# An encoder block on one core: four chunks of the conditioning weight summed in the branch stage, the first by one-row products, and the first norm's modulation through PSUM

## The chip, the cores and the metric

The kernel runs on one core of a Trainium2 chip. A core has four compute engines, each with its own in-order queue: TensorE (PE) multiplies matrices into PSUM, VectorE (DVE) and ScalarE (ACT) work on SBUF and PSUM, GpSimd (POOL) on SBUF. SyncE (SP) issues the DMAs, in order too. The metric is the device time of one execution in microseconds; the median of several runs is compared. Before the change it is 1581.42 us (three runs, 1576.99 to 1583.48).

## The reference, cut to what matters

One encoder layer with D = 1024, S = 1024 positions, batch 1, in float32. Six vectors of 1024 elements, made from a conditioning vector c, scale, shift and gate the stream:

```python
ada = jax.nn.silu(c) @ w_ada[i] + b_ada[i]            # (1024) @ (1024, 6144)
shift1, scale1, gate1, shift2, scale2, gate2 = jnp.split(ada, 6, axis=-1)
h = rmsnorm(x, g_mix[i]) * (1 + scale1) + shift1
proj = h @ w_in[i]                                    # q, k, v of two attentions, two gates
...
merged = jax.nn.sigmoid(ga) * ya + jax.nn.sigmoid(gb) * yb
x = x + gate1 * (merged @ w_out[i])
h2 = rmsnorm(x, g_ffn[i]) * (1 + scale2) + shift2
u = depthwise_conv_seq(h2 @ w_up[i], conv_w[i], conv_b[i])
...
x = x + gate2 * ((jax.nn.gelu(u_gate, approximate=True) * u_val) @ w_down[i])
return rmsnorm(x, g_final)
```

So shift1 and scale1 are needed before the first projection, gate1 at the output projection, shift2 and scale2 at the second norm, gate2 only at the very end.

## The kernel before

Everything is kept transposed: features on the 128 partitions, in KT = 8 blocks k, and positions along the free dimension, in two halves of 512. A float32 product is made of three fp32r products, from operands that were split into a high part (ACT rounds a copy) and a low part (the rest, by DVE or POOL): L77 to L79 for 512 columns, L247 to L249 for the 256-column v products. The stages, in order of time: start (norm1, first q, k and v products), v stage (the rest of v for both attentions), two attentions with the gate projections, branch stage (both branch products, gates, merge), output projection, norm2, the wide feed-forward products, the end.

**w_ada.** It is 24 MB and comes as 12 chunks j of 512 columns, each [128, 8, 512], in four tiles of two rows t (512 KB). A chunk is a sum over 8 rows, each scaled by a column of cs (silu of c, one value per partition), then a sum over partitions. `ada_rows` (L155, L157) does the sum over rows on DVE, in place; `ada_sums` (L141) turns each 128 columns into a column of PSUM by a product with `ones`, or with a column of cs where a row was not scaled; it is 4 products, 8 records in a profile, to a tile named pada. `ada_bias` adds the bias. Chunks 0 to 3 hold shift1 and scale1, chunk q those for k = 2q and 2q + 1, so that norm1 can go on in four steps. Chunks 4 and 5 hold gate1, 6 and 7 shift2, 8 and 9 scale2, 10 and 11 gate2.

**The start** is written out by hand for all engines (`manual_schedule`). ACT squares x's half 0, DVE adds the squares, PE sums them over partitions (L91), `norm_bcast` makes the reciprocal root and PE spreads it over partitions as `pb` in PSUM (L104). Chunk 0 is summed by ACT and POOL for three rows (`ada_rows_pool`), by DVE for four, joined by `ada_join`, with the eighth row by PE from the unscaled weights. `to_sbuf` (L201) copies pb for POOL, `scale_x` (L206) multiplies x by it on DVE or POOL, and `modulate` makes h from a scaled x: its high part on ACT (L212, scale and bias), the full value on DVE (L214) and the low part (L215). Four steps q follow, each with a chunk's sums, two k of modulation, the q and k products of these (`qk_products`, 12 products of 512 columns) and the v products (24 of 256). Their weights are split in two halves by `qk_split` and `v_split` on ACT, POOL and DVE. Half 1 of x is loaded in step 3, then squared and modulated in the same manner.

**The v stage.** After the hand-written block the planner orders the instructions, by its own estimate of times; on each engine that order is then fixed. For both attentions (br) and both halves of v's columns (hv) there are eight products of 128 positions, each copied out by ACT and written to memory (L255); more copies in memory rearrange v for the attentions (L457, L459, L481). Chunks 4 and 5 stand at the end of the hand-written block, and in the loop over (br, hv) two more follow each time, 6 to 11. Their tiles come from a pool of four buffers ("wada", 4 KB per partition).

**The branch stage** is written out by hand for all engines too: 16 iterations i (8 output blocks m, two halves). Each issues the loads of gates i + 2 (a tile of three) and of a block of x, on even i the weights of m + 2; ACT does the sigmoid of gates i + 1; PE makes 2 x 12 products into two banks of PSUM, "pj", of which there are six; DVE multiplies the first with one gate (L821), the second with the other (L822), adds (L823), and ACT and DVE split the sum into m's high and low part (L55, L56). The operands come from `o_operands`, which loads 8 tiles for each branch through four buffers, "oraw", and splits each into its parts on ACT and DVE.

## Time and profile before

| | us |
|---|---|
| median of the runs | 1581.42 |
| profiled execution, its own time | 1584.16 |
| span of that execution's trace | 1582.3 |
| PE busy in the first 205 us | 161.78 |
| PE busy in the branch stage, 725 to 809 us | 84.00 |
| DVE busy in the branch stage | 43.65 |

The profile is of one execution; times within it count from its first instruction. A row of the timeline or of a group names the source line, the engine, the operation, and the tiles written and read; x8 is a count of instructions, and what stands in brackets at the end is the idle time of the engine before it, with what ended it. The chain of waits goes back from the last instruction, at each step to what released it; "issue" there is time for which the profile shows no cause. A window's row has the busy time and the count of each engine, the clock that TensorE was granted (1.00 is full), the share of time that the DMA engines were busy and the rate in GB/s. A busy PE can be at half rate: then a product of 512 columns follows the last after 0.43 us, at full rate after 0.23.

### The profile page before, as it was taken

To read this page: it belongs to the slowest core of one execution; us is meant where nothing else is said; L and a number is where in the kernel's file an instruction comes from. 1 tells how busy PE (TensorE), PEld (TensorE's weight loads), DVE (VectorE), ACT (ScalarE), POOL (GpSimd) and SP (SyncE) were. 2 spreads that over 40 slices of the span, in tenths; PEclk is the share of its full clock that TensorE was granted. 3 is DMA by queue.
4 is the path that set the end of the run, shared out by engine and by line. 5 is a ranking of instruction groups with operands and counts; after the bars stand their busy time and mean duration, and the time that the engine had idled before them with its cause. 6 is when DMAs were issued, how large, how long until landed. Compare 5 with 4: busy or idle time off the path is not lost.

```text
span 1582.3 us, 21932 instructions
## 1 busy us (share of the span) xinstructions
PE 1502.5 (95%) x7884; PEld 1284.6 (81%) x7884; DVE 1046.1 (66%) x1872; ACT 815.1 (52%) x1463; POOL 837.1 (53%) x523
## 2 busy tenths in 40 slices
PE   4897989999999999999999899999999999999998
PEld 3797978888888989888888777788888887778788
DVE  6876455676757667544433899876666667887765
ACT  4531165766676677654335354444444446575542
POOL 4562052535344575521246758676666665678711
PEclk9898989999999999999999999999999999999998
DMA  6747832222223344446534212222222223533313
GB/s 230 263 148 276 273 104 69 85 72 79 82 70 120 103 126 132 148 161 226 187 139 160 94 53 80 93 95 80 80 80 82 90 75 141 168 118 122 112 54 107
DMA packets 113268, 196.86 MB, mean 124 GB/s; under 512 B 40072, under 2 KB 61448, under 8 KB 113160
## 3 DMA queue, kind: packets, MB, share of 16 engines
q1 hardware_dynamic: 112888, 195.20, 37.2%
q8 instruction: 62, 1.02, 0.3%
q14 instruction: 46, 0.38, 0.1%
q10 hardware_dynamic: 272, 0.26, 0.1%
HBM read 158.73 MB, written 42.47 MB: 127 GB/s over the span
## 4 chain that ended last, share of the span: by engine, by line
PE 75%; DVE 12%; ACT 4%; issue 3%; DMA 2%; POOL 2%; SPq 1%; DVEq 0%; ACTq 0%; POOLq 0%
PE pj L885 10%; PE pj L886 10%; PE pj L884 10%; PE pj L77 9%; PE pj L78 9%; PE pj L79 9%; PE pj L402 2%; DVE big L1080 2%; PE pv L249 2%; PE pv L247 2%; PE pv L248 2%; PE O L716 2%; PE T L704 1%; PE S L683 1%; PE O L571 1%
## 5 line engine op out<-in xcount | busy, mean ns | idle before, releaser
L56 POOL TENSOR_TENSOR wlo<-wraw,whi 128x1024 fp32r<-128x1024 f32 (+2 forms) x78 | 180.3, 2311 | 273.4 <-ACT whi L55 229.5
L77 PE MATMUL pj<-h,whi 128*128 128x512 f32 x448 | 180.4, 404 | 8.5 <-ACT h L212 6.7
L78 PE MATMUL pj<-h,whi 128*128 128x512 f32 x448 | 180.7, 403 | 2.2 <-DVE h L215 2.1
L79 PE MATMUL pj<-h,wlo 128*128 128x512 f32 x448 | 180.3, 402 | 0.0
L56 POOL TENSOR_TENSOR wsl<-big,wsh 128x1024 fp32r<-128x1024 f32 (+1 forms) x45 | 110.0, 2447 | 47.9 <-ACT wsh L55 47.8
L1080 DVE SCALAR_TENSOR_TENSOR big<-wc,sm,big 128x256 f32<-128x256 f32 (+1 forms) x132 | 119.1, 950 | 17.3 <-ACT big L1074 17.2
L55 ACT ACTIVATE whi<-wraw 128x1024 fp32r<-128x1024 f32 (+2 forms) x81 | 81.2, 1003 | 87.3 <-PE pj L78 45.3
L77 PEld LDWEIGHTS pj<-h,whi 128*128 128x128 f32 x448 | 85.8, 192 | 24.5 <-ACT h L212 7.0
L78 PEld LDWEIGHTS pj<-h,whi 128*128 128x128 f32 x448 | 86.0, 192 | 18.2 <-DVE h L215 3.2
L79 PEld LDWEIGHTS pj<-h,wlo 128*128 128x128 f32 x448 | 85.9, 192 | 15.8
L542 ACT ACTIVATE P<-P,st 128x256 f32<-128x256 f32 x128 | 64.4, 504 | 45.9 <-DVE st L541 45.0
L541 DVE CUSTOM_DVE_ANT_0 P<-S,bias 128x256 f32<-128x256 f32 x128 | 51.8, 421 | 51.4 <-PE S L588 37.3
L157 DVE SCALAR_TENSOR_TENSOR wada<-wada,cs 128x512 f32<-128x512 f32 x67 | 64.9, 969 | 30.5 <-DMA wada<-w_ada 28.5
L429 POOL TENSOR_SCALAR kl<-kl 64x512 fp32r<-64x512 f32 x32 | 63.5, 1983 | 33.1 <-DVE kl L427 30.2
L1080 DVE SCALAR_TENSOR_TENSOR big<-pj,sm,big 128x512 f32<-128x512 f32 x132 | 67.8, 564 | 16.4 <-ACT big L1074 16.4
L1074 ACT ACTIVATE big<-wc,sm 128x512 f32<-128x512 f32 x44 | 35.8, 817 | 76.3 <-DVE wc L897 45.9
L247 PE MATMUL pv<-vwh,h 128*128 128x256 f32 x256 | 74.6, 292 | 0.0
L249 PE MATMUL pv<-vwh,h 128*128 128x256 f32 x256 | 74.4, 291 | 0.0
L248 PE MATMUL pv<-vwl,h 128*128 128x256 f32 x256 | 73.3, 287 | 0.0
L56 POOL TENSOR_TENSOR wsl<-wraw,wsh 128x768 fp32r<-128x768 f32 (+1 forms) x23 | 49.9, 2168 | 43.8 <-ACT wsh L55 43.8
L474 POOL TENSOR_TENSOR vv<-vv 96x256 fp32r<-96x256 f32 (+2 forms) x32 | 41.0, 1292 | 51.9 <-ACT vv L473 47.6
L694 POOL TENSOR_SCALAR P<-P,stb 128x288 f32<-128x288 f32 (+1 forms) x32 | 39.4, 1231 | 53.6 <-DVE stb L691 41.8
(365 smaller groups left out, 4928.2 us busy)
## 6 DMA issues: line engine op xcount, KB each, us to landing
wada<-w_ada SPq DMA_DIRECT2D x47, 512.0 KB, 5.5
wraw<-w_in SPq DMA_DIRECT2D x36, 512.0 KB, 4.3
big<-w_up SPq DMA_DIRECT2D x22, 512.0 KB, 5.2
wraw<-w_up SPq DMA_DIRECT2D x22, 512.0 KB, 3.6
as<-big SPq DMA_DIRECT2D x22, 512.0 KB, 2.9
big<-as SPq DMA_DIRECT2D x22, 512.0 KB, 6.0
wraw<-w_down SPq DMA_DIRECT2D x24, 384.0 KB, 4.2
gs<-gs SPq DMA_DIRECT2D x32, 256.0 KB, 2.0
```

The costliest lines, as they stand in the source:

```text
L55: act.activation(hi, raw, AF.Copy)
L56: lo_eng.tensor_tensor(lo, raw, f(hi), OP.subtract)
L77: pe.matmul(psum, whi[:, k0 + k], mhi, start=k == 0, stop=False)
L78: pe.matmul(psum, whi[:, k0 + k], mlo, start=False, stop=False)
L79: pe.matmul(psum, wlo[:, k0 + k], mhi, start=False, stop=k == n - 1)
L247: pe.matmul(p, hhi, hi[:, k], start=fresh and k == 0, stop=False, skip_group_check=True)
L248: pe.matmul(p, hhi, lo[:, k], start=False, stop=False, skip_group_check=True)
L249: pe.matmul(p, hlo, hi[:, k], start=False, stop=k == KT - 1, skip_group_check=True)
L884: pe.matmul(psum, whi[:, k], bhi, start=j < 4 and k == 0, stop=False, skip_group_check=True)
L885: pe.matmul(psum, whi[:, k], blo, start=False, stop=False, skip_group_check=True)
L886: pe.matmul(psum, wlo[:, k], bhi, start=False, stop=k == n - 1, skip_group_check=True)
L1080: dve.scalar_tensor_tensor(y[:, dst], src, wt, y[:, dst], OP.mult, OP.add)
```

## The change

- Chunk 0 is summed by PE: `ada_gemv` takes a column of cs as stationary operand and a float32 row of w_ada, 512 columns, as moving one, and adds eight of them into one row of a PSUM bank, `grow`. ACT copies that row to SBUF, and four products with one row of contraction turn it into pada's columns. In PE's queue the first two stand ahead of the square sums, two between these and the transposes of `norm_bcast`, four behind.
- In chunks 1 to 3 DVE sums rows 0 to 4, and PE takes rows 5, 6 and 7 unscaled (three more products of `ada_sums` for each 128 columns). ACT's and POOL's part and the joins are gone.
- `modulate` starts from the unscaled x: DVE writes x times (1 + scale) g times pb to a PSUM bank (two banks in turn, `stages1`), ACT makes the high part from it with the shift as bias, and DVE the low part in one operation. `scale_x` and `to_sbuf` are gone. All of it is on DVE and ACT; the low parts of the first q, k and v weights are all on POOL.
- The 16 tiles of chunks 0 to 3 have places of their own, in buffers that q, k and v operands use later, and so their loads wait for none. On SP, x's half 1, the second v load and chunk 4 follow them directly. All of x is in the pool of h tiles, and the pool "mt" has three buffers instead of four.
- Chunks 4 and 5 leave the hand-written block for the planner. In the loop of the v stage only 8 and 9 remain, one for each hv of the first attention.
- Chunks 6, 7, 10 and 11 are summed in the branch stage, row by row: 32 loads of 256 KB through o_operands' four buffers, two issued ahead and two more in each iteration behind gates and x; two additions on DVE in each iteration, ahead of its products with the gates, into PSUM ("pcol"); and after every fourth iteration's products `ada_sums` on PE and the bias on DVE.

The diff, cut to its core:

```diff
--- before.py
+++ after.py
...
-
-    slots = iter(range(1 << 20))
+    grow = ps_s.tile([128, 512], FT, name="pv", bufs=3)
+
+    homes = iter([(qkpool, "kl", 3)] + [(qkpool, n, b) for n, b in (("qs", 3), ("ks", 3), ("qb", 2))
+                                        for _ in range((3, 3, 1)[("qs", "ks", "qb").index(n)])]
+                 + [(early, "wada", 3)] * 2 + [(adapool, "wada", 4)] * 4 + [(qkpool, "qb", 2), (early, "wada", 3)])
 
     def wada_tile(j):
-        n = next(slots) if j < 4 else -1
-        if n == 0:
-            return qkpool.tile([128, 2, 512], FT, name="kl")
-        if n > 0 and (n - 1) % 6 < 2:
-            return early.tile([128, 2, 512], FT, name="wada", bufs=2)
-        return adapool.tile([128, 2, 512], FT, name="wada", bufs=4)
+        p, name, bufs = next(homes, (adapool, "wada", 4))
+        return p.tile([128, 2, 512], FT, name=name, bufs=bufs)
 
     def ada_load(j):
 
...
-    def ada_sums(parts, pa=None, stop=True, n=4):
+    def ada_sums(parts, pa=None, stop=True, n=4, new=None):
 
         first = pa is None
-        pa = ps_s.tile([128, 4], FT, name="pada", bufs=1) if first else pa
+        if first:
+            pa = new if new is not None else ps_s.tile([128, 4], FT, name="pada", bufs=1)
         for i, (w, col) in enumerate(parts):
             for m in range(n):
                 pe.matmul(pa[:, m:m + 1], w[:, m * 128:(m + 1) * 128], col, start=first and i + m == 0,
...
-    def ada_rows_pool(wt, ts):
+    def ada_gemv(rows, ts):
+
         for t in ts:
-            act.activation(wt[t], wt[t], AF.Copy, scale=cs[:, t:t + 1])
-        for t in ts[1:]:
-            pool.tensor_tensor(wt[ts[0]], wt[ts[0]], wt[t], OP.add)
-
-    def ada_join(wt, a, b):
-        dve.tensor_tensor(wt[a], wt[a], wt[b], OP.add)
+            pe.matmul(grow[0:1], cs[:, t:t + 1], rows[t], start=t == 0, stop=t == KT - 1)
 
     def ada_chunk(j, wt):
         ada_rows(wt, range(KT))
...
@@ -196,23 +192,18 @@
     def norm_bcast(pcol):
         return bcast(rstd_of(pcol, 4), ps_n, "pbc")
 
-    def to_sbuf(pb):
-        bc = early.tile([128, 512], FT, name="mt", bufs=4)
-        act.activation(bc, pb, AF.Copy)
-        return bc
-
-    def scale_x(x, pb, bc, ks, e):
-        for k in ks:
-            e.tensor_tensor(x[k], x[k], pb if e is dve else bc, OP.mult)
-
-    def modulate(x, hf, ks, lo_eng):
-        for k in ks:
-            a, b = am1[:, k:k + 1], ada[:, k:k + 1]
-            hi, lo = h[hf, k] = h_tile(), h_tile()
-            act.activation(hi, x[k], AF.Identity, bias=b, scale=a)
-            t = early.tile([128, 512], FT, name="mt", bufs=4)
-            dve.tensor_scalar(t, x[k], a, b, OP.mult, OP.add)
-            lo_eng[k % 2].tensor_tensor(lo, t, f(hi), OP.subtract)
+    def modulate(x, hf, ks, pb):
+
+        last = ()
+        for k in [*ks, None]:
+            if k is not None:
+                hi, lo = h[hf, k] = h_tile(), h_tile()
+                t, b = stages1[k % 2], ada[:, k:k + 1]
+                dve.scalar_tensor_tensor(t, x[k], am1[:, k:k + 1], pb, OP.mult, OP.mult)
+                act.activation(hi, t, AF.Identity, bias=b)
+            if last:
+                dve.scalar_tensor_tensor(*last, OP.add, OP.subtract)
+            last = k is not None and (lo, t, b, f(hi))
 
     def v_load(br, hv):
         return [w_load(w_in[(8, 20)[br] + 2 * hv + t]) for t in range(2)]
@@ -288,68 +279,59 @@
     with tc.manual_schedule(engines={e.engine for e in (sp, act, dve, pool, pe)}):
         x = [x_load(0)]
         sp.dma_start(sm, small)
-        wt = {0: ada_load(0)}
+        wt = [ada_load(0)]
         qk_raw = [wpool.tile([128, KT, 128], FT, name="wraw") for _ in range(2)]
         half_load(qk_raw, (0, 4), 0)
         v_raw = [qkpool.tile([128, KT, 128], FT, name="kl") for _ in range(2)]
         half_load(v_raw, (8, 9), 0)
-        wt[1] = ada_load(1)
-        wt[2] = ada_load(2)
+        wt.append(ada_load(1))
+        wt.append(ada_load(2))
         half_load(qk_raw, (0, 4), 1)
         half_load(v_raw, (8, 9), 1)
-        wt[3] = ada_load(3)
+        wt.append(ada_load(3))
+        x.append(x_load(1))
+        v_raw1 = v_load(0, 1)
+        ada_w = ada_load(4)
         qk_w = [[wpool.tile([128, KT, 128], FR, name=n) for n in ("whi", "wlo")] for _ in range(2)]
         v_w = [v_tiles()]
         qk_psum = [ps_g.tile([128, 512], FT, name="pj") for _ in range(2)]
 
         accs = sq_accs()
         square(x[0], accs, range(8), dve)
+        ada_gemv(wt[0], range(2))
         pcol = square_sums(accs)
+        ada_gemv(wt[0], range(2, 4))
         pb = norm_bcast(pcol)
-        ada_rows_pool(wt[0], range(3))
-        ada_rows(wt[0], range(3, 7))
-        ada_join(wt[0], 3, 0)
-        bc = to_sbuf(pb)
-        pa = ada_sums([(wt[0][7], cs[:, 7:8]), (wt[0][3], ones)])
-        scale_x(x[0], pb, None, range(2), dve)
-        qk_split(0, (pool, dve))
-        v_split(v_raw, (pool, dve), slice(0, 4), v_w[0])
-        scale_x(x[0], pb, bc, range(2, 4), pool)
-        piece_bias(0, pa)
-        modulate(x[0], 0, range(2), (dve, dve))
-        qk_products(range(2))
+        ada_gemv(wt[0], range(4, 8))
+        row = early.tile([128, 512], FT, name="mt", bufs=3)
+        act.activation(row[0:1], grow[0:1], AF.Copy)
+        pa = ps_s.tile([128, 4], FT, name="pada", bufs=1)
+        for m in range(4):
+            pe.matmul(pa[:, m:m + 1], row[0:1, m * 128:m * 128 + 128], ones[0:1], start=m == 0, stop=m == 3,
+                      skip_group_check=True)
+        stages1 = [ps_n.tile([128, 512], FT, name="pcol"), grow]
+        qk_split(0, (pool, pool))
+        v_split(v_raw, (pool, pool), slice(0, 4), v_w[0])
         pvs = [v_banks()]
-        ada_rows_pool(wt[1], range(3))
-        for q in range(1, 4):
-            ks, c = range(2 * q - 2, 2 * q), 2 * q
-            p = (0, 3, 4, 4)[q]
-            ada_rows(wt[q], range(p, (8, 7)[q > 1]))
-            ada_join(wt[q], p, 0)
-            pa = ada_sums([(wt[q][7], cs[:, 7:8])], stop=False) if q > 1 else None
+        for q in range(4):
+            ks = range(2 * q, 2 * q + 2)
+            piece_bias(q, pa)
+            modulate(x[0], 0, ks, pb)
+            qk_products(ks)
+            if q < 3:
+                ada_rows(wt[q + 1], range(5))
             v_products(0, (0, 1), ks)
-            pa = ada_sums([(wt[q][p], ones)], pa)
+            if q == 1:
+                qk_split(1, (pool, pool))
+                v_split(v_raw, (pool, pool), slice(4, 8), v_w[0])
+            if q < 3:
+                pa = ada_sums([(wt[q + 1][t], cs[:, t:t + 1]) for t in range(5, 8)], stop=False)
             v_products(0, (2, 3), ks)
-            if q == 1:
-                scale_x(x[0], pb, bc, range(4, 6), pool)
-            if q == 2:
-                qk_split(1, (pool, dve))
-                v_split(v_raw, (pool, dve), slice(4, 8), v_w[0])
-                scale_x(x[0], pb, bc, range(6, 8), pool)
             if q < 3:
-                ada_rows_pool(wt[q + 1], range(4))
-            else:
-                x.append(x_load(1, range(4)))
-                v_raw1 = v_load(0, 1)
-                x[1] += x_load(1, range(4, 8))
-                accs = sq_accs()
-                square(x[1], accs, range(3), dve)
-            piece_bias(q, pa)
-            modulate(x[0], 0, range(c, c + 2), (dve, dve))
-            qk_products(range(c, c + 2))
-        v_products(0, range(4), range(6, 8))
+                ada_sums([(wt[q + 1][0], ones)], pa)
         v_w.append(v_split(v_raw1, (dve, pool)))
-        ada_w = ada_load(4)
-        square(x[1], accs, range(3, 8), dve)
+        accs = sq_accs()
+        square(x[1], accs, range(8), dve)
         for st in range(4):
             v_out(0, 0, st, pvs[0][st])
         pvs.append(v_banks())
@@ -358,15 +340,13 @@
         v_products(1, (1,), range(8))
         pb = norm_bcast(pcol)
         v_products(1, (2, 3), range(8))
-        bc = to_sbuf(pb)
-        scale_x(x[1], pb, bc, range(0, 8, 2), dve)
-        scale_x(x[1], pb, bc, range(1, 8, 2), pool)
-        modulate(x[1], 1, range(4), (dve, pool))
+        stages1 = [ps_n.tile([128, 512], FT, name="pcol"), ps_s.tile([128, 512], FT, name="pv", bufs=3)]
+        modulate(x[1], 1, range(8), pb)
         for st in range(4):
             v_out(0, 1, st, pvs[1][st])
-        modulate(x[1], 1, range(4, 8), (dve, pool))
-        ada_chunk(4, ada_w)
-        ada_chunk(5, ada_load(5))
+
+    ada_chunk(4, ada_w)
+    ada_chunk(5, ada_load(5))
 
     def qk_tiles(br, pr, ws=None, ps=None):
         qt, kt = ((0, 4), (12, 16))[br]
@@ -490,10 +470,8 @@
                     v_out(br, hv, st, v_product(st, w))
             if br == 0:
                 va_chunks(slice(hv * 256, hv * 256 + 256))
-            for j in range(2):
-                jj = 6 + 4 * br + 2 * hv + j
-                if jj < 12:
-                    ada_chunk(jj, ada_load(jj))
+            if br == 0:
+                ada_chunk(8 + hv, ada_load(8 + hv))
     dve.scalar_tensor_tensor(am2, ada[:, 32:40], 1.0, g_ffn, OP.add, OP.mult)
     work.release()
     adapool.release()
@@ -794,8 +772,29 @@
         o.append(o_operands(1, work))
         sp_order.close()
         sp_order.enter_context(tc.manual_schedule(engines={e.engine for e in (sp, act, dve, pool, pe)}))
+        late = [(j, t) for j in (6, 7, 10, 11) for t in range(KT)]
+        rows, sums = {}, {}
+
+        def row_load(n):
+            j, t = late[n]
+            rows[n] = opool.tile([128, 512], FT, name="oraw", bufs=4)
+            sp.dma_start(rows[n], w_ada[j][:, t])
+
+        def row_add(n):
+            j, t = late[n]
+            w, col = rows.pop(n), cs[:, t:t + 1]
+            if t == 0:
+                sums[j] = ps.tile([128, 512], FT, name="pcol")
+                dve.tensor_scalar(sums[j], w, col, None, OP.mult)
+            else:
+                dst = w if t == KT - 1 else sums[j]
+                dve.scalar_tensor_tensor(dst, w, col, sums[j], OP.mult, OP.add)
+                sums[j] = dst
+
         for i in range(2):
             gate_load(i)
+        for n in range(2):
+            row_load(n)
         ws[0] = w_split(w_raw[0], pool)
         act.activation(gates[0], gates[0], AF.Sigmoid)
         for i in range(2 * KT):
@@ -813,10 +812,17 @@
                 act.activation(gates[i + 1], gates[i + 1], AF.Sigmoid)
             if hf == 0:
                 ws[m + 1] = w_split(w_raw[m + 1], pool)
+            for n in range(2 * i + 2, min(2 * i + 4, 32)):
+                row_load(n)
+            for n in range(2 * i, 2 * i + 2):
+                row_add(n)
             p = []
             for br in range(2):
                 p.append(ps.tile([128, 512], FT, name="pj", bufs=6))
                 product(p[br], ws[m], lambda k: [t[:, k, cols] for t in o[br]], 4 * br, 4)
+            if i % 4 == 3:
+                j = late[2 * i][0]
+                ada_bias(4 * j, ada_sums([(sums.pop(j), ones)], new=ps.tile([128, 512], FT, name="pbc")))
             g = gates.pop(i)
             dve.tensor_tensor(g[:, 0], p[0], g[:, 0], OP.mult)
             dve.tensor_tensor(p[1], p[1], g[:, 1], OP.mult)
```

More of the change, by code (lines that the diff above doesn't have):

```diff
@@ L174, in x_load @@
         for k in ks:
-            x.append(early.tile([128, 512], FT, name="xl", bufs=1) if hf + k == KT else h_tile(FT))
+            x.append(h_tile(FT))
             sp.dma_start(x[-1], xT[k][:, halves[hf]])
```

2 lines of the change are left out of this document (1 added, 1 removed).

## The prediction

> **What bounds the kernel now.** First the page: where the busy time is.
>
> ```profile
> span 1582.3 us, 21932 instructions
> PE 1502.5 (95%) x7884; PEld 1284.6 (81%) x7884; DVE 1046.1 (66%) x1872; ACT 815.1 (52%) x1463; POOL 837.1 (53%) x523
> ```
>
> TensorE (PE) is the bound; of its 79.8 us idle, the windows by stage put over half before the attention:
>
> ```profile
> 0.00:205.00 205.00, 161.78 (x1082) 151.15 (x1082) 134.11 (x175) 70.20 (x120) 77.00 (x53) 0.92 0.70 237
> 725.00:809.00 84.00, 84.00 (x369) 68.92 (x368) 43.65 (x65) 31.28 (x39) 19.23 (x8) 1.00 0.56 179
> ```
>
> The columns are busy us of PE, PEld, DVE, ACT, POOL, then granted clock, DMA share, GB/s. The first 205 us leave PE idle 43.2 us; the branch stage (725 to 809) leaves it nothing, so there any work put on PE lengthens the kernel, while DVE has half its time free. The chain of waits says what PE idles for in the first stage:
>
> ```profile
> 122.28 7.18 issue
> 129.47 1.83 PE pada L141 x8
> ...
> 132.79 0.21 PE pv L249
> ...
> 136.82 0.13 PE pv L247
> 143.31 0.79 PE pada L141 x8
> ...
> 156.31 1.57 issue
> ...
> 189.51 4.06 DMA vbc<-vs
> ...
> 197.19 4.82 DMA bias<-p_bias
> ```
>
> At 122.28 PE stands before the sums of a w_ada chunk (pada). The views of waits name what is behind it, and the last stall:
>
> ```profile
> SPq L131 <- DVE wada L157: 30.8, 11, 8.6
> PE S L557 <- DVE st L541: 6.8, 1, 6.8
> DMA to landing us min/median/max: 3.4/5.5/9.8
> ```
>
> The w_ada loads wait for their four buffers (freed by DVE's row sums), then take 5.5 us to land (the last row is of the loads from w_ada alone), and PE waits in order behind them. After the 7.18 us the 256-column products take 0.21 us apiece where they take 0.12 to 0.13 otherwise: half rate until 136.8.
>
> **The change, part by part.**
>
> *1. The v stage (86 to 195 us) loses chunks 6, 7, 10 and 11.* Before, eight chunks (4 to 11) pass there; after, four. Gone: the stall of 7.18 us, the one of 1.57, the half-rate stretch behind the first (129.5 to 136.8, 7.3 us of which half, 3.65, is lost), and four sums of 0.79 (3.2). Together 15.6. Chunks 5, 8 and 9 still pass the four buffers (one per about 13 us: the sums at 129.47 and 143.31 lie 13.8 apart), some 40 us in a stage of 95, and the planner may again put a sum ahead of its data. I take 14 off; bounds 3.2 (only the sums go) and 15.6.
>
> *2. Behind the v stage.* PE's 6.8 us at the attention's start wait for a bias load issued at 197.19, queued on SP behind the v copies, whose last v write went out at 189.51 and took 4.06. Three or four w_ada issues leave this stretch of SP's queue and the DMAs are emptier: I take 2; bounds 0 and 6.8.
>
> *3. The start.* What sets it now:
>
> ```profile
> kl<-w_ada SPq DMA_DIRECT2D x1, 512.0 KB, 7.2
> 6.09 0.70 SPq L131 DMA_DIRECT2D kl<-w_ada  x1
> 13.42 1.86 PE L91 MATMUL pcol<-ones,sq 128*128 128x1 f32 x8 [0.95 <-DVE sq L188]
> 17.46 0.57 ACT L201 ACTIVATE mt<-pbc 128x512 f32<-128x512 f32 x1
> 27.06 1.52 ACT L212 ACTIVATE h<-h,ada,am 128x512 fp32r<-128x512 f32 x2 [6.50 <-DVE am L265]
> 27.93 0.79 PE L77 MATMUL pj<-h,whi 128*128 128x512 f32 x1 [3.82 <-ACT h L212]
> 59.95 0.43 PE pj L79
> 69.16 0.23 PE pj L78
> 69.46 0.28 PE L247 MATMUL pv<-vwh,h 128*128 128x256 f32 x1
> 85.87 0.62 PE L77 MATMUL pj<-h,whi 128*128 128x512 f32 x2
> ```
>
> Chunk 0's first tile lands at 6.09 + 7.2 = 13.3, and the first two one-row products stand in PE's queue ahead of the square sums (before at 10.6 and 13.42). No row shows an f32 product of 512 columns. Four f32 products of one column are eight records, so the weights go in two parts. Below, one pass for each part: 2 x 0.43 = 0.86 us at half rate, 0.46 at full; above, two passes for each part: 1.72 and 0.92. I take the upper, since the kernel itself needs three products for an f32 product in two parts without the smallest. By the Trainium skill, page "FP8 and Floating Point Precision", section "TensorE Precision Notes", a true f32 product takes four passes, which gives the upper price too; no run here shows it yet.
>
> What goes with chunk 0's old way (ACT's scalings, POOL's and DVE's additions, the copy of the broadcast, the scaling of x) is replaced by this chain, and with chunks 1 to 3 DVE sums five rows and PE takes three. The loads that waited for buffers now have tiles of their own and leave in one run; x's half 1 is ahead on SP of the second v load, which waits for the first weight tiles' splits, with chunk 4 behind it. Nobody waits for these two before half 1, so I cost that at nothing; without this cover it is one load, 5.5.
>
> So: 13.3 + 2 x 1.72 = 16.7; square sums 2 x 1.86 gives 20.4 at half rate (19.5 if full rate comes meanwhile); products 2 and 3, 21.3; transposes 0.6; four more, 25.6; ACT's copy of the row 0.57 and eight records of the turn into columns 0.8 give 27.2 with gaps; DVE's bias 0.35 and first product 0.75, ACT's 0.8: first product at 29.2, 1.3 later than 27.93. By the lower price it is 25.5, where ACT's splits, now behind the row copy, hold it. Then four steps. One has on PE 12 products of 0.23 (2.8), 24 of 0.12 (2.9), four sums of 0.8 (3.2) and 1.9 of waiting (bias 0.35, product 0.75, ACT 0.8): 10.8. DVE has 4 x 0.75 + 0.35 + 0.48 and four row sums, inside that at 0.76, just outside at 1.73 (what the row sums take alone and with POOL at work):
>
> ```profile
> 16.34 0.76 DVE wada L157
> 17.13 1.73 DVE wada L157
> ```
>
> Sum: 29.2 + 3 x 10.8 + 5.7 + 1 for that = 68.3. Before, the same point is 69.46 + 2.9 = 72.3. From there to the first product of half 1 it is 13.6 us before, the same v products, square sums and transposes after; but the squares on ACT now come only behind the last step and the v split, for which I allow 1.6. DVE's 16 x 0.75 = 12 us of modulation then keeps about even with PE's 1.4 per k. So 83.5 against 85.87. I take 2.3 off; bounds 6 off and 4 more (one-row products at half rate throughout, and idle gaps of 1.9 that bring half rate back).
>
> *4. The branch stage* gets 32 row loads of 256 KB, 32 DVE operations and four sums.
>
> ```profile
> 717.55 0.39 PE L77 MATMUL pj<-o0hi,whi 128*128 128x512 f32 x1
> 720.82 1.45 DVE L56 TENSOR_TENSOR o1lo<-oraw,o1hi 128x512 fp32r<-128x512 f32 x2 [9.74 <-ACT o1hi L55]
> ...
> 726.18 0.69 DVE L56 TENSOR_TENSOR o1lo<-oraw,o1hi 128x512 fp32r<-128x512 f32 x1 [1.12 <-ACT o1hi L55]
> ...
> 739.72 0.70 DVE L822 TENSOR_TENSOR pj<-pj,g 128x512 f32<-128x512 f32 x1 [2.06 <-PE pj L79]
> ...
> 741.82 0.69 DVE L56 TENSOR_TENSOR mlo<-pj,mhi 128x512 fp32r<-128x512 f32 x1 [0.67 <-ACT mhi L55]
> 742.47 0.69 DVE L821 TENSOR_TENSOR g<-pj,g 128x512 f32<-128x512 f32 x1
> 745.21 0.70 DVE L822 TENSOR_TENSOR pj<-pj,g 128x512 f32<-128x512 f32 x1 [2.06 <-PE pj L79]
> 811.13 0.75 DVE L1016 SCALAR_TENSOR_TENSOR x<-pj,ada,x 128x512 f32<-128x512 f32 x1 [2.70 <-PE pj L79]
> 743.76 2.40 POOL L56 TENSOR_TENSOR wlo<-wraw,whi 128x1024 fp32r<-128x1024 f32 x1 [6.39 <-ACT whi L55]
> 721.69 0.32 SPq L778 DMA_DIRECT2D oraw<-ob  x1
> DMA to landing us min/median/max: 2.7/3.8/5.0
> g<-gs SPq DMA_DIRECT2D x11, 512.0 KB, 4.0
> ```
>
> PE's beat is 5.49 (739.72 to 745.21), and DVE waits 2.06 + 0.67 of it. Two row additions at 0.75 (L1016: one operand in PSUM, as here) fill 1.5 of the 2.06: 5.0 of 5.49, no loss in the steady state. Whether POOL's 2.40 us split, one in two iterations, slows them to 1.73 is the question; both operands in SBUF did so at 17.13, but here one is in PSUM, and L821 to L823 keep 0.70 in every iteration. The Trainium skill, "SBUF — State Buffer", section "Who interferes with whom", says that a DVE instruction with at most one SBUF input doesn't contend with GpSimd; by that the price is 0.75; by the other row DVE would need 3.5 + 2.1 + 1.4 = 7.0 in half of the iterations, and the stage some 8 us more.
>
> The four sums stand on a full PE: 4 x 0.8 = 3.2. The first comes too early. The row tiles use o_operands' four buffers; the fifth to eighth tile of branch 1 free them at 722.3 to 726.9 (DVE's rows above). Row 0 is issued at 722.3 and lands at 726.1 (3.8 is the oraw loads' median), row 1 at 727.7; behind them on SP now stand the load of the third w_br tile, the third gates and x. DVE's iteration 0, before at 724.4, ends its additions at 728.4 and then runs at 5.0 each: 733.4, 738.4, so iteration 3's additions end near 743.4. PE's iteration 3 ends at 717.55 + 4 x 5.49 = 739.5 and the sum of chunk 6 waits behind it: 3.9 us, with all later products queued behind. Bounds 0 and 8. For an idle time of that size there is a row: after 3.3 us idle ending at 38.7 the granted clock is half,
>
> ```profile
> 38.00:40.00 2.00, 1.23 (x6) 1.26 (x7) 0.67 (x1) 0.00 (x0) 1.84 (x3) 0.50 0.18 49
> ```
>
> and 3.65 us went that way at 129.5; I add 2 (not sure to happen). The branch stage: 3.2 + 3.9 + 2 = 9.1 more. The other three sums follow a DVE that is back in step (additions done 4.3 after PE's last product, PE needs them at 5.49).
>
> *Sum:* -14 - 2 - 2.3 + 9.1 = -9.2, on the profiled execution's 1584.16: 1575.0. That execution is 2.74 above the median of 1581.42, so against the median 1572.2.
>
> **Rivals.**
>
> *All covers hold:* rows in time for the first sum (branch +3.2), start 6 off, v stage 15.6, tail 3: -21.4, 1560.0. For it: the planner places what isn't ordered by hand, and the one-row price is unknown. Against: row 0 cannot leave before its buffer is free.
>
> *The v stage keeps its stall:* only the sums go (3.2), no gain behind it: -3.2 - 2.3 + 9.1 = +3.6, 1585.0, no change. For it: the same four buffers and a fixed order on PE. Against: half the chunks.
>
> *Row loads set the beat (slower):* rows of iteration i+1 are issued once DVE ends iteration i-1 and frees a gate tile, 1.4 us into SP's queue; landing L, additions 1.5, three multiplications 2.1 and gaps 0.2 make 5.2 + L for two iterations, against 10.98. It decides from L = 5.8. The gates' 512 KB take 4.0 and the DMAs are 0.56 busy, which the rows raise by 512 KB in 5.49 us (95 GB/s on 179). At 9.8, the longest a w_ada load took anywhere, 7.5 a beat: 13 x 2.0 = 26 more, -9.2 + 26 = +17, 1598.
>
> *The start gets worse:* 4 later instead of 2.3 earlier: -2.9, 1578.5, no change.
>
> **How the numbers follow.** Forecast 0.42, covers hold 0.28, v stall 0.13, beat 0.10, start 0.07. The forecast's own range is 1567 to 1578. 0.5% is 7.9 us, about what can be told from no change. Faster: 0.28 and 0.26 of the forecast's 0.42, 0.54; same: 0.16 of it, 0.10 and 0.05, 0.31; slower 0.15. Range 1560 to 1584: the fast rival's time below, up to nearly the v rival's above.
>
> **What would show it.** Right: no "issue" over 2 us in the chain from 85 to 180; first half-1 product near 83.5; one PE gap of about 4 us before a pada in the branch stage near its fourth iteration, the beat 5.49 from then. Wrong: the beat above 5.49 with DVE waiting for row DMAs; one-row products under 1 us at half rate; PE waiting for pada in the v stage again; a first product after 31.

## The result, and the profile after

The kernel after takes 1607.63 us (median; 1601.83 to 1609.99), against 1581.08 for the kernel before: a ratio of 1.0158 (95% 1.0129 to 1.0186), 1.6% slower. The forecast was 1572.2. The profiled execution of after took 1601.83. Its page:

```profile
span 1600.0 us, 21951 instructions
PE 1516.2 (95%) x7948; PEld 1289.0 (81%) x7948; DVE 1007.9 (63%) x1862; ACT 803.5 (50%) x1448; POOL 803.6 (50%) x503
```

The two traces lie 17.7 us apart (spans of 1582.3 and 1600.0), less than the ratio's 25, since after's is of its fastest execution. In them PE's busy time grew by 13.7 us, its idle time by only 4.0 (79.8 to 83.8). Busy time holds products at half rate too, so the windows come next (us busy of PE, PEld, DVE, ACT, POOL, then granted clock, DMA share, GB/s):

```profile
0.00:205.00 205.00, 163.97 (x1074) 146.42 (x1075) 79.68 (x127) 59.46 (x109) 48.26 (x35) 0.89 0.59 193
40.00:80.00 40.00, 26.35 (x152) 22.83 (x151) 27.90 (x42) 8.80 (x14) 6.81 (x5) 0.80 0.48 159
725.00:809.00 84.00, 79.97 (x354) 65.40 (x353) 58.67 (x88) 30.11 (x39) 16.85 (x7) 0.98 0.84 272
```

From 40 to 80 us PE is busy for 26.35 of 40 us, before 35.06. The chain of waits of after shows what it stands for there:

```profile
13.32 3.50 PE pv L162 x4
16.82 1.88 PE pcol L91 x16
18.70 1.81 PE pv L162 x4
...
21.08 3.54 PE pv L162 x8
...
28.74 0.79 PE pj L77
...
50.40 0.76 DVE wada L157
51.21 3.62 DMA wada<-w_ada
...
58.48 0.67 DVE wada L157
59.16 3.70 DMA wada<-w_ada
62.88 1.42 DVE wada L157 x2
64.33 3.72 DMA wada<-w_ada
...
69.70 3.54 DMA wada<-w_ada
...
74.91 3.54 DMA wada<-w_ada
...
96.94 5.77 DMA wada<-w_ada
```

The chain goes through loads of w_ada, six of them between 51 and 103 us. DVE's rows and these loads take turns in it: two rows end at 64.30 and free a buffer, the load into it leaves at 64.33 and takes 3.72, and the next rows wait for it. The first product comes at 28.74, close to the 29.2 of the forecast; what goes wrong in the start of this execution comes later. DVE's timeline names the loads' waiters, by line: in the rows shown L155 and L157 are row sums of chunks 4 and 5, L254 is a step's bias, L202 a modulation:

```profile
54.95 0.49 DVE L155 TENSOR_SCALAR wada<-wada,cs 128x512 f32<-128x512 f32 x1 [3.81 <-DMA wada<-w_ada]
55.48 0.75 DVE L157 SCALAR_TENSOR_TENSOR wada<-wada,cs 128x512 f32<-128x512 f32 x1
56.15 0.15 DVE L254 TENSOR_TENSOR ada<-pada,sm 128x4 f32<-128x4 f32 x1
...
68.14 1.54 DVE L157 SCALAR_TENSOR_TENSOR wada<-wada,cs 128x512 f32<-128x512 f32 x2 [2.51 <-DMA wada<-w_ada]
70.71 0.48 DVE L155 TENSOR_SCALAR wada<-wada,cs 128x512 f32<-128x512 f32 x1 [1.03 <-DMA wada<-w_ada]
71.23 0.75 DVE L157 SCALAR_TENSOR_TENSOR wada<-wada,cs 128x512 f32<-128x512 f32 x1
73.34 1.54 DVE L157 SCALAR_TENSOR_TENSOR wada<-wada,cs 128x512 f32<-128x512 f32 x2 [1.36 <-DMA wada<-w_ada]
74.80 0.15 DVE L254 TENSOR_TENSOR ada<-pada,sm 128x4 f32<-128x4 f32 x1
...
105.83 0.75 DVE L202 SCALAR_TENSOR_TENSOR pcol<-h,am,pbc 128x512 f32<-128x512 f32 x1
```

The bias of the fourth step (74.80) stands in DVE's queue behind rows that wait for their loads. Nothing in the step needs these rows; they were put there when chunks 4 and 5 left the hand-written block and the planner placed them by its own estimate. The steps come 14 to 19 us apart (biases at 26.43, 40.60, 56.15 and 74.80) instead of the 10.8 forecast, and half 1's modulation begins at 105.83, where the kernel before reached it at 81.04.

### The profile page after: what moved, and what is told of

Its sections match the earlier page's. It is cut to its first block, busy times and chain, and to the rows that moved or that the text cites. A ratio compares the mean times of both kernels' runs of the same rounds, so it can differ in the third digit from the quotient of the medians.

```text
span 1600.0 us, 21951 instructions
## 1 busy us (share of the span) xinstructions
PE 1516.2 (95%) x7948; PEld 1289.0 (81%) x7948; DVE 1007.9 (63%) x1862; ACT 803.5 (50%) x1448; POOL 803.6 (50%) x503
## 4 chain that ended last, share of the span: by engine, by line
PE 72%; DVE 12%; DMA 5%; ACT 3%; POOL 3%; issue 3%; SPq 0%; DVEq 0%; POOLq 0%; ACTq 0%
PE pj L77 10%; PE pj L78 10%; PE pj L79 10%; PE pj L891 9%; PE pj L890 9%; PE pj L892 9%; DVE big L1086 2%; PE pj L382 2%; DMA wada<-w_ada 2%; PE O L694 2%; DVE wada L157 1%; POOL wsl L56 1%; DMA wraw<-w_down 1%; PE T L682 1%; PE pv L238 1%
## 5 line engine op out<-in xcount | busy, mean ns | idle before, releaser
L55 ACT ACTIVATE wsh<-big 128x1024 fp32r<-128x1024 f32 (+1 forms) x45 | 44.8, 1000 | 37.6 <-POOL big L855 23.1
L1112 ACT ACTIVATE big<-big 128x1024 f32<-128x1024 f32 x22 | 23.3, 1060 | 79.6 <-DVE big L1086 79.5
```

The costliest lines, as they stand in the source:

```text
L55: act.activation(hi, raw, AF.Copy)
```

## The experiments

All ratios are to the kernel before, which took 1580.1 to 1582.9 us (medians) beside them; 0.5% is 7.9 us. A ratio is formed over the runs and can differ a little from the quotient of the two medians: for the first experiment below that quotient is 1.0055, the ratio 1.0040.

**Chunks 4 and 5 back in the block of the kernel after.**

```diff
-
-    ada_chunk(4, ada_w)
-    ada_chunk(5, ada_load(5))
+        ada_chunk(4, ada_w)
+        ada_chunk(5, ada_load(5))
```

> The changed kernel with one edit undone: chunks 4 and 5 are summed at the end of the hand-written block again, not where the planner puts them. Order theory (their row sums, and those of 8 and 9 behind them, stand in DVE's queue ahead of the start's own steps and each waits for its load): no DMA wait of a row sum between 45 and 80 us, half 1's modulation starts near 80 us instead of 105.8, and the kernel takes 1580 to 1590 us instead of 1607. Start theory (the one-row products and DVE's whole modulation are slow by themselves) and branch theory (the late first sum and the fuller DMAs): 1600 or more, as the changed kernel.

1588.77 us, ratio 1.0040 (1.0022 to 1.0059): 1.18% of 1580, about 19 us, are the price of the release in the new start. The time is as the order theory had it; half 1's modulation starts at 92.33, earlier than 105.83 but not near 80. DVE waits for no load of w_ada among the steps any more (one wait of 1.8 us is left in the first 130, behind half 1's modulation), and its longest waits are now for PE's sums:

```profile
DVE ada L254 <- PE pada L141: 18.7, 3, 6.9
DVE ada L254 <- PE pada L310: 9.1, 1, 9.1
DVE rs L96 <- PE pcol L91: 8.8, 2, 7.2
```

**The release alone, on the kernel before** (the reverse of that edit).

> The kernel before with that one edit made: chunks 4 and 5 leave the hand-written block. Order theory: slower than before, but by less than the whole, since here they can only mix with half 1's squares and modulation: 4 to 12 us. Start and branch theories: no difference from before.

1575.11 us, 0.9958 (0.9939 to 0.9978): faster, against the expectation. In the old start chunk 4 is loaded only behind the second v load, and the planner's rows begin among half 1's squares, behind the four steps. So the release as such isn't slow; it depends on where the rows fall.

**The branch move alone, on the kernel before** (chunks 6, 7, 10, 11, with the branch stage's code as in the change).

> The kernel before with chunks 6, 7, 10 and 11 moved to the branch stage and nothing else. Branch theory: 15 to 25 us slower than before. Order theory: the branch stage costs about 5 us and the v stage gains 10 to 15, so 5 to 10 us faster than before, 1571 to 1577.

1580.14 us, 0.9992 (0.9972 to 1.0012): no change, and neither theory's number. PE's waits of the first 220 us still have the stall that was to go with the chunks:

```profile
PE pada L142 <- issue: 11.4, 2, 7.0
```

**The kernel after with these four chunks back in the v stage.**

> The changed kernel with chunks 6, 7, 10 and 11 back in the v stage. Order theory and start theory: 1600 or more, as the changed kernel, since the start is as late. Branch theory: back to 1580 to 1587.

1609.86 us, 1.0175 (1.0143 to 1.0208), as the kernel after within the intervals. The branch move as a whole isn't where the time was lost.

**Release and branch move together, on the kernel before.**

> The old start, with chunks 4 and 5 released from the hand-written block (alone 0.9958 of before) and chunks 6, 7, 10 and 11 in the branch stage (alone 0.9992). If the two parts only add, 1573 to 1577 us. Theory: the move of the chunks gained 9 us up to the branch stage although the 7.0 us stall of the v stage stayed, and gave it back there; with the rows of chunks 4 and 5 begun earlier the stall goes too, and the time is 1566 to 1572. Rival: without the row sums of chunks 4 and 5 in the block and with fewer chunks after, nothing is left that the release gains, and the time is that of the branch move alone, 1578 to 1582.

1586.56 us, 1.0041 (1.0028 to 1.0054): a miss. The two don't add (0.9958 and 0.9992 alone). PE has a wait of 7.4 us for ACT's copy of a v bank that neither edit has alone (1.0 with the branch move, none with the release), and ACT waits for the writes of earlier copies (first PE's wait in the first 260 us, then ACT's from 85 to 165 us):

```profile
PE pv L248 <- ACT vs L255: 8.5, 2, 7.4
```

```profile
ACT vs L255 <- DMA vas<-vs: 15.9, 3, 8.9
```

Why the order of these writes changes so was not tried.

**All rows of chunks 1 to 3 on DVE, chunks 4 and 5 in the block.**

```diff
-                ada_rows(wt[q + 1], range(5))
+                ada_rows(wt[q + 1], range(KT))
...
-                pa = ada_sums([(wt[q + 1][t], cs[:, t:t + 1]) for t in range(5, 8)], stop=False)
...
-                ada_sums([(wt[q + 1][0], ones)], pa)
+                pa = ada_sums([(wt[q + 1][0], ones)])
```

> The new start with chunks 4 and 5 in the hand-written block (1588.8), and all eight rows of chunks 1 to 3 added up by VectorE, so that TensorE folds one row of four products per chunk, not four rows. Theory: TensorE sets the steps of the new start, and the nine rows that it folds besides cost what they take there: 5 to 8 us less, 1581 to 1584. Rival: VectorE sets the steps; nine more row additions of 0.75 to 1.6 us in its queue make it 1592 to 1600.

1580.00 us, 0.9994 (0.9980 to 1.0007): less than with PE's folds by 8.8 us in the medians and by 0.0046, some 7 us, in the ratios, about what the theory had. DVE's wait for these sums falls from 18.7 to 5.9 us. DVE had the time, and PE had not.

**Norm1's modulation through PSUM alone, on the kernel before** (`modulate` and `stages1` as in the change, `scale_x` and `to_sbuf` removed).

> The kernel before with nothing changed but norm1's modulation, which goes through PSUM as in the kernel after (two operations of VectorE and one of ScalarE per tile, no scaled copy of x). Theory: the modulation itself does not cost, and spares VectorE and GpSimd work: 1573 to 1581. Rival: the chain VectorE, ScalarE, VectorE over two PSUM banks is what makes the new start slow: 1586 to 1592.

1566.86 us, 0.9923 (0.9904 to 0.9943), faster than expected and faster than both kernels. Its first product, and the start of half 1's modulation:

```profile
24.80 0.79 PE L77 MATMUL pj<-h,whi 128*128 128x512 f32 x1 [2.18 <-ACT h L216]
...
72.47 0.76 DVE L215 SCALAR_TENSOR_TENSOR pcol<-h,am,pbc 128x512 f32<-128x512 f32 x1 [1.82 <-PE pbc L104]
```

They stand at 27.93 and 81.04 before. So this part of the change is worth some 12 us, and the rest of the change loses more than that.

**Chunk 4 in the block of the kernel after, chunk 5 still released.**

> The kernel after with chunk 4 at the end of the hand-written block again, and only chunk 5 (and those behind it) released. Theory: each released row that lands among the steps of the start waits there for its load, so the cost goes with the number of rows that do: between 1588.8 and 1607.6, some 1593 to 1602. Rival: chunk 4's rows alone do the harm, 1586 to 1591. Second rival: any released chunk does all of it, 1604 to 1610.

1587.63 us, 1.0054 (1.0033 to 1.0075): the first rival. The harm doesn't go with the number of rows; it hangs on where chunk 4 stands. Half 1's modulation starts at 91.98 (92.33 with both in the block), and no row of chunk 5 stands ahead of it. In the kernel after rows of chunk 5 do stand among the steps (70.71 and 73.34 above), so this run doesn't show that chunk 4's rows alone do the harm. The reading that fits: its tiles come from the buffers of chunk 4, so while chunk 4 stands at the end of the block none behind it can come earlier.

**The other parts of the change, each alone beside the modulation (0.9923).** First the one-row products for chunk 0, in the place that they have in the change; the splits of the first weights kept their two engines, POOL and DVE:

> The old start with norm1's modulation through PSUM (1566.9 us alone), and besides only the first chunk as one-row products on TensorE, placed as in the kernel after. Theory: these products end later than the row sums that VectorE, ScalarE and GpSimd shared, so the first product of the projections starts at some 28.7 us as in the kernel after, not at 24.8, and the kernel takes 3 to 6 us more: 1570 to 1573. Rival: the three engines that are freed bring the next chunk forward and win it back, 1562 to 1568.

1575.80 us, 0.9972 (0.9952 to 0.9993), some 8 us more than the modulation alone and more than the theory's 3 to 6. The first product was later than the theory had it:

```profile
35.55 0.79 PE L77 MATMUL pj<-h,whi 128*128 128x512 f32 x1 [4.81 <-ACT h L222]
```

Then chunks 1 to 3 with five rows on DVE and three folded by PE:

> The old start with norm1's modulation through PSUM (1566.9 us alone), and besides only chunks 1 to 3 summed as in the kernel after: five rows by VectorE, three folded by TensorE, none by ScalarE and GpSimd. Theory: VectorE adds the rows behind the step's modulation, with TensorE's folds behind them, and each of the three steps grows by 2 to 4 us: 1573 to 1579. Rival: ScalarE's and GpSimd's share was hidden work, and the new way costs only the folds: 1566 to 1570.

1575.11 us, 0.9973 (0.9956 to 0.9989), some 8 us more than the modulation alone, in the theory's range. The window from 40 to 80 us, first with the modulation alone, then with this:

```profile
40.00:80.00 40.00, 37.23 (x261) 34.24 (x260) 30.62 (x44) 21.46 (x38) 15.07 (x12) 0.96 0.68 243
```

```profile
40.00:80.00 40.00, 35.51 (x203) 31.89 (x203) 26.58 (x36) 15.08 (x28) 7.95 (x6) 0.80 0.57 205
```

PE is busy nearly as long and issues 58 records fewer, at a clock of 0.80 instead of 0.96: it idles longer (4.5 us instead of 2.8; its waits for ACT's high part grow from 4.4 to 8.1 us in the first 260), and it works at half rate for part of the time.

Then the branch move:

> The old start with norm1's modulation through PSUM (1566.9 us alone), and besides only chunks 6, 7, 10 and 11 in the branch stage. Theory: as with the kernel before, what the v stage gains is given back in the branch stage: 1564 to 1569. Rival: with the earlier start the v stage's stalls (5.6 and 2.8 us) go with the chunks, and half of what the v stage gains stays: 1556 to 1562.

1569.99 us, 0.9939 (0.9918 to 0.9960): 0.16% over the modulation alone, the two intervals overlap. The weight loads of branch stage and output projection bound the branch stage, first without the move, then with it:

```profile
L77 PEld LDWEIGHTS pj<-o0hi,whi x64: 187/188/188, 700.2 to 784.6; 128*128 128x128 f32 x64
...
L77 PEld LDWEIGHTS pj<-mhi,whi x128: 187/188/192, 788.1 to 878.1; 128*128 128x128 f32 x128
```

```profile
L77 PEld LDWEIGHTS pj<-o0hi,whi x64: 187/188/331, 698.9 to 788.2; 128*128 128x128 f32 x64
...
L77 PEld LDWEIGHTS pj<-mhi,whi x128: 187/188/192, 791.7 to 882.6; 128*128 128x128 f32 x128
```

The stage grows from 87.9 to 92.8 us, and before its first product there is a wait for ACT's gs. The other kernels with the move have it too, with 3.4 to 6.2 us (the last experiment 1.4), those without the move don't:

```profile
698.92 0.80 PE L77 MATMUL pj<-o0hi,whi 128*128 128x512 f32 x1 [4.22 <-ACT gs L727]
```

Without that wait the stage would begin at 694.7, 5.5 earlier than without the move: this is what the earlier stages gained, and 4.2 + 4.9 = 9.1 is what the branch stage cost.

Last the release:

> The old start with norm1's modulation through PSUM (1566.9 us alone), and besides only chunks 4 and 5 released from the hand-written block. Theory: in the old start chunk 4 is loaded after the fourth step's rows, so its rows fall only among half 1's squares and modulation, and the release gains some 5 us as with the kernel before: 1560 to 1564. Rival: half 1's modulation now lies on VectorE alone, and the rows among it hold it up as in the kernel after: 1572 to 1585.

1574.86 us, 0.9963 (0.9951 to 0.9975), 6 us slower, where the same edit had gained 6.6 with the old modulation. DVE has half 1's modulation alone now, and the rows stand in it one by one, as the rival said; it lasts from 75.75 to 99.33, with the modulation alone from 72.47 to 84.26:

```profile
77.06 0.74 DVE L157 SCALAR_TENSOR_TENSOR wada<-wada,cs 128x512 f32<-128x512 f32 x1
77.72 0.74 DVE L218 SCALAR_TENSOR_TENSOR h<-pcol,ada,h 128x512 fp32r<-128x512 f32 x1
78.39 0.73 DVE L157 SCALAR_TENSOR_TENSOR wada<-wada,cs 128x512 f32<-128x512 f32 x1
```

**One-row products with the splits ahead of the row's copy** (edited from the run with the modulation and the one-row products).

```diff
+        qk_split(0, (pool, pool))
+        v_split(v_raw, (pool, pool), slice(0, 4), v_w[0])
         row = early.tile([128, 512], FT, name="mt", bufs=4)
...
-        qk_split(0, (pool, dve))
-        v_split(v_raw, (pool, dve), slice(0, 4), v_w[0])
         piece_bias(0, pa)
```

> As the kernel with the modulation through PSUM and the first chunk as one-row products (1575.8 us), but the first weight splits stand ahead of the copy of the summed row in ScalarE's queue, and their second halves are GpSimd's, not VectorE's. In that run VectorE stood 9.3 us at a split that waited for ScalarE's copy, and the first product started at 35.5 us. Theory: the splits' place cost most of that; the first product starts at 28 to 29.5 us and 3 to 6 us remain over the modulation alone: 1570 to 1573. Rival: the products themselves (and the half clock that they run in) cost it, 1574 to 1578. Second rival: the engines that they free win it back, 1563 to 1568.

1573.27 us, 0.9945 (0.9925 to 0.9966): 3.5 us over the modulation alone, between it and the 7.7 us of the other order, and its interval overlaps with both. The time is as the theory had it, the first product isn't: it comes at 32.95. The place of the splits isn't why; they end at 23.33, and the row's copy waits for the one-row products:

```profile
29.30 0.59 ACT L325 ACTIVATE mt<-pv 1x512 f32<-1x512 f32 x1 [5.97 <-PE pv L172]
```

In the kernel after the copy starts at 24.71. The square sums take 3.57 us here and about 1.9 there, and so do the two one-row products behind them: PE came to its full rate later in this execution. The order of the splits does show in the first product, 35.55 against 32.95 (DVE's bias stands behind two splits there and runs at 33.64, here at 31.03), but the two times lie within each other's intervals.

**No row of chunk 4 ahead of the end of the four steps, in the kernel after.**

```diff
+        ada_rows(ada_w, range(1))
         accs = sq_accs()
         square(x[1], accs, range(8), dve)
...
-    ada_chunk(4, ada_w)
+    ada_rows(ada_w, range(1, KT), ada_w[0])
+    ada_bias(16, ada_sums([(ada_w[0], ones)]))
```

> The kernel after, with the first row of chunk 4 put behind the four steps of half 0 in the hand-written block, and the rest released as in it: no row of chunk 4 or 5 can stand among the four steps, but they still stand among half 1's squares, norm and modulation. Theory: the steps lost 5 us to the rows (the fourth came 18.7 us behind the third, 13.8 with both chunks in the block), the stretch from there to half 1's modulation the rest (30.8 against 18.5 us): 1600 to 1605. Rival: the rows among the steps carry the loss, since they delay all that follows: 1588 to 1595.

1595.49 us, 1.0084 (1.0062 to 1.0105), 0.74% or 12 us less than after: just above the rival's range, clearly under the theory's. By the times, rows among the four steps make some 12 of the 19 us, those among half 1's squares and modulation the other 7. The start of half 1's modulation, 99.27, lies between 105.83 and 92.33 too, but counted from the first step's bias it is 72.6 against 79.4 and 62.9, which gives the first kind less than half. So the 19 us are firmer than their split.

**The first two rows of the branch stage loaded later**, with the modulation and the branch move.

```diff
-        for n in range(2):
-            row_load(n)
...
-            for n in range(2 * i + 2, min(2 * i + 4, 32)):
+            for n in range(2 * i + 2 * (i > 0), min(2 * i + 4, 32)):
```

> The kernel with the modulation through PSUM and the branch move (1570.0 us), with the first two row loads of the branch stage put behind the first iteration's gate and x loads. Theory: the branch stage's added time is a wait of 4.2 us at its beginning: a bank's copy by ScalarE stands behind two splits of operands whose loads are late, because the row loads share the operands' four buffers and come early in SyncE's list. With ScalarE's order of before again, that wait goes and the stage takes 88 to 89.5 us, not 92.8: 1565 to 1568. Rival: the four sums and VectorE's late iterations of 7.7 us carry it: 1569 to 1572.

1572.01 us, 0.9938 (0.9918 to 0.9958), not told from 0.9939 and so not the theory's gain. Its stage, the wait in front included, takes 96.1 us instead of 97.0. The wait for ACT shrinks, and the wait that the forecast had named takes its place (PE's waits from 690 to 810 us):

```profile
PE pbc L142 <- DVE oraw L808: 2.3, 1, 2.3
PE pj L77 <- ACT gs L727: 1.4, 1, 1.4
```

## Why the prediction was wrong

The parts nearly add up. Beside the modulation (0.9923) the one-row products cost 0.0049, the shared rows 0.0050 and the branch move 0.0016, together 1.0038, where the run with all four measured 1.0040; the release of chunks 4 and 5 adds 0.0118, to after's 1.0158. That the fit is so close is luck: each ratio is known to about 0.002, with the splits placed otherwise the products cost 0.0022, and the earlier loads in places of their own, which are in the run with all four, were not tried alone. The forecast was 9.2 us less, the ratio says 25 us more: a miss of some 34 us.

1. **The failed step: "Nobody waits for these two before half 1, so I cost that at nothing"** (with "without this cover it is one load, 5.5"). This looked at who waits for chunk 4's load. It did not look at what is queued behind the instructions that wait for it. Out of the hand-written block, chunk 4's eight rows and those behind it could be placed anywhere on DVE's queue, and they were placed among the steps. Their loads weren't there: the first left at 51.21, when a row of chunk 2 had freed its buffer, each took 3.5 us or more, and the biases of the third and fourth step stood behind rows that waited for them, for up to 3.81 us. With both chunks back in the block 0.0118 of the time is gone: the term costs 19 us, not nothing. No rival had it either: "the start gets worse" reached 4 us later, by PE's rate.

2. **The start, forecast at -2.3.** The price of the one-row products was right, the upper one: two of them took 3.50 us at half rate (1.75 each) and four 3.54 at full (0.89), against 1.72 and 0.92. (The clock column has 1.00 for both; the half rate is read from the products' own lengths.) The first product, 28.74 against 29.2, was right by luck as well: with the same code up to there, it comes at 28.95 and 29.01 in two other traces, but at 31.73, 31.84 and 33.20 in three, in which the square sums and the next two products still ran at half rate (3.57 us or more each). The forecast's bound of 4 us more held this case. By the Trainium skill, "FP8 and Floating Point Precision", section "TensorE Precision Notes", a true f32 product takes four passes; the trace agrees, 1.75 against 0.43 for one product in fp32r at half rate. What was wrong is the reference for it: with the modulation through PSUM and chunk 0 summed as before, the first product comes at 24.80 to 26.33 in five traces, so the one-row products took 2 us or more of the modulation's gain. The steps of 10.8 us were wrong too, even with both chunks in the block, where the four biases lie 14.5, 15.7 and 13.8 apart: the sum had PE busy for 8.9 us and waiting for 1.9, with all DVE work inside; PE's folds instead stand between the row sums and the bias, and after the idle time PE runs at half rate (0.72 from 40 to 80 us). With the release undone the kernel is at 1.0040; less the 0.0016 of the branch move that leaves, if the parts add, some 4 us more for the start, not 2.3 less.

3. **The v stage (-14) and behind it (-2).** From half 1's modulation to the attention's first product the branch move gained 13.8 us on the kernel before (127.6 to 113.8) and 7.7 with the modulation (120.4 to 112.7). Of this 6.6 and 4.0 are the wait at the attention's start (6.8 to 0.2, 4.0 to nothing): the forecast had 2 for it. That leaves 7.2 and 3.7 for the v stage, not 14, since the stall stayed: 7.0 us with the kernel before, and of the two waits with the modulation the longer was 6.1. The rival "the v stage keeps its stall" was right on this, and the gain behind the stage, which that rival left out, was larger than forecast. Chunks 4, 5, 8 and 9 still follow each other through four buffers, and PE's order still puts a sum ahead of its data. In the kernel after itself this stall is gone, but PE waits 7.0 us for ACT's copies of the v banks; with chunks 4 and 5 back in the block the stall is there again, with 6.4.

4. **The branch stage (+9.1): the size held by luck, one term didn't.** Its 9.1 with the modulation are the four sums (3.2), 1.7 that fit the lower clock (0.91 from 700 to 720 us, which loses 1.8), and 4.2 us in front, a wait that the forecast didn't have. In after, too, PE stands 4.03 us before its first product, for ACT's copy of a bank, which stands behind two operand splits whose loads are late. ACT's and PE's timelines of after:

```profile
726.61 0.63 ACT L55 ACTIVATE o1hi<-oraw 128x512 fp32r<-128x512 f32 x1 [3.75 <-DMA oraw<-ob]
727.76 0.63 ACT L55 ACTIVATE o1hi<-oraw 128x512 fp32r<-128x512 f32 x1 [0.52 <-DMA oraw<-ob]
728.30 1.04 ACT L55 ACTIVATE whi<-wraw 128x1024 fp32r<-128x1024 f32 x1
729.25 0.58 ACT L710 ACTIVATE gs<-pj 128x512 f32<-128x512 f32 x1
```

```profile
729.88 0.71 PE L77 MATMUL pj<-o0hi,whi 128*128 128x512 f32 x1 [4.03 <-ACT gs L710]
```

The "late first sum" of 3.9 us did not occur there: the stage begins later, by which time the rows are in. It came, at 2.3, only where the rows were loaded later. The beat of 5.49 held (DVE's second gate product at 765.64 and 771.13), so the rival "row loads set the beat" fell. DVE's rows in after took what was chosen (shortest, median and longest, in ns):

```profile
L791 DVE SCALAR_TENSOR_TENSOR pcol<-oraw,cs,pcol x24: 744/756/757, 735.7 to 819.8; 128x512 f32<-128x512 f32 x24
```

None took longer than 757 ns, but that tells little: POOL's splits overlap with one row in each second iteration, for 0.2 to 0.5 us. The gate product, with one operand in PSUM too, says more: at 759.34 it took 0.69 us under a split (759.23 to 761.64), 0.68 elsewhere. That agrees with the Trainium skill, "SBUF — State Buffer", section "Who interferes with whom", by which a DVE instruction with at most one SBUF input, outside the two-port modes, doesn't contend with GpSimd.

What stays open: why the release and the branch move together cost the kernel before 6 us where neither does alone; what the remaining stall of the v stage would need to go; what the earlier loads are worth; why PE came to its full rate at some 17 us in some executions and behind 24 in others; and by which estimate the planner put the rows where they were.

## What to carry to other kernels

When work leaves a hand-written order for a planner, don't ask only who waits for that work; ask what it can be put in front of on an in-order queue, and whether its data are there by then. One edit can have either sign: the same release gained 6.6 us with one modulation and lost 6 with another. And try the parts of a change alone: here one of them, the modulation through PSUM, was worth 0.8%, and the others together cost three times that.

## What the runs showed of the hardware

Little was unexpected. DVE row sums with both inputs in SBUF took 0.75 us, and 1.65 to 1.67 from 45.34 to 50.4 us of the kernel after, where POOL split weights (43.72 to 49.81). A chunk's first row, which has one such input (L155), took 1.47 us beside the split, at 43.83, and 0.48 alone, at 60.37. In the branch stage DVE's fourth iterations took 7.7 us instead of 5.5 (the first gate product at 716.60, 724.30 and 729.03 with the modulation and the branch move), and PE waited for none of them; that its six banks of PSUM held the delay is the reading that fits.
